# A two-layer diffusion backbone: the next norm's shift and scale move from TensorE, in the attention, to VectorE, at the output projection

## The chip, the cores and the metric

One core of one Trainium2 chip runs the whole program. The metric is the device time of one execution in microseconds (us); three runs of the kernel before are shown, and one further execution was profiled.

## The reference

The even layer is all that the change touches. Its conditioning vector `c` gives six modulation vectors of 1024 values each: shift, scale and gate of the mixer, and shift, scale and gate of the FFN.

```
sh1, sc1, g1, sh2, sc2, g2 = ada_params(c, w_ada[i], b_ada[i])   # silu(c) @ w_ada + b_ada, split in 6
h_lat = modulate(rmsnorm(x_lat, g_mix[i]), sh1, sc1)              # h * (1 + scale) + shift
o_lat, o_ctx = hybrid_mixer(h_lat, h_ctx, ...)                    # attention and Fourier mixing, one output projection
x_lat = x_lat + g1 * o_lat
h = modulate(rmsnorm(x_lat, g_ffn[i]), sh2, sc2)
x_lat = x_lat + g2 * conv_ffn(h, w_up[i], ...)
```

`x` has 512 tokens of 1024 features; the change concerns how `sh2` and `sc2` of layer 0 are computed. All is float32.

## The kernel before

Tokens lie in four row tiles of 128 (`t`), features in eight k tiles of 128 (`kt`). A float32 product is made of three passes on values split into a high and a low part (`mm3`, L222 to L226). Weights of the large products come as 128x1024 chunks in one order through `Stream`: SP loads a chunk into `st` (two buffers), ScalarE casts the high part `whi` (L196), VectorE subtracts to get `wlo` (L197); five chunks are held, and a chunk's buffers come free when TensorE has used it last. The instructions of each engine, and SP's list of loads, stand in an order that a scheduler fixes when the program is built; each engine works its own list from front to back.

The stages around the change, in `mixer` (L889):

- **Attention** (L807): 8 units of a row tile and a key head; in each, four heads with scores (L820), the row maximum on VectorE (L822), the exponential on ScalarE (L825), a division on GpSimd (L828), then transposes of the probabilities (L837), their split into two parts (L290, L291) and the value products (L842).
- Beside it runs a filler, `sums` (L907). For each of gate, shift and scale it makes a `Block` (L320): 8 chunks of `w_ada` (512 KB each, `sa` and `sx`) are loaded in two halves of four, TensorE multiplies each half with the conditioning column `cT` (L340, four groups of 32 output rows), ScalarE and VectorE add the halves in `gs` (L343, L345), and TensorE turns the rows into a column (L350, `col`). The gate's column is spread over all rows (`in_every_row`, L404, L405); shift and scale go to `S2` and `A2` (`in_rows`, L411 and L409), a value for each partition and k tile.
- **Output projection**, `token_major` (L862): the first 512 output columns of all row tiles in one loop over the k tiles (Fourier features first), into the two-bank accumulators `D`; then the last 512 columns, row tile by row tile, into `B`. `residual` (L457) multiplies with the gate and adds to `x` (L460, L461). After each row tile's second half `fin` (L487) normalises it: a sum of squares on ScalarE (L490), the root through L286 on VectorE and L287 on GpSimd, the scaling to `xs` on VectorE (L492). After each pair of row tiles `features` (L469) transposes `xs` on TensorE (L477), applies `A2` and `S2` on ScalarE (L482) and splits the result into `h` on VectorE (L484, L485).
- **FFN** (L939): its first products (`first_blocks`) take the first pair's `h` as it comes. Beside the FFN, other modulation vectors are computed without TensorE: `ada_sum` (L413) loads a chunk of `wada` (L418), and VectorE multiplies it with the activated conditioning row `scb` and sums along it in one instruction (L420). `silu_rows` (L304) makes `scb`: one load to all partitions and a Silu on ScalarE (L307, L308).

`token_major` takes a filler too and runs `n_fill` of its steps after each k tile of the first loop; here it gets none:

```
with sbuf("xs") as xp:
    token_major("wo", (4, 5, 6, 7, 0, 1, 2, 3), gate1, finisher(xp, A2, S2), chain(), 0)
```

The pool `xs` is opened when the attention's pools are closed, and takes their memory.

Of the kernel before, what the change touches and what calls it, by code (L numbers as in the profile page):

```python
# [10 lines left out]
F32 = mybir.dt.float32  # L11
# [6 lines left out]
P = 128  # L18
D = 1024
SEQ = 512  # L20
CTX = 256
KT = D // P
# [199 lines left out]
def mm3(nc, out, lhs, rhs, start, stop):  # L222
    (lh, ll), (rh, rl) = lhs, rhs
    nc.tensor.matmul(out, lhsT=lh, rhs=rh, start=start, stop=False)  # L224
    nc.tensor.matmul(out, lhsT=lh, rhs=rl, start=False, stop=False)  # L225
    return nc.tensor.matmul(out, lhsT=ll, rhs=rh, start=False, stop=stop).ins  # L226
# [3 lines left out]
def tile_hybrid_backbone(ctx: ExitStack, tc: tile.TileContext, x_in, ctx_in, vecs_in, gains_in, cond_in, condT_in, wada, wnat,  # L230
# [10 lines left out]
    def sbuf(name, side="left"):  # L241
        return tc.tile_pool(name=name, bufs=1, side=side, reuse_waits="tile")
# [3 lines left out]
    def nm(s):  # L246
        uid[0] += 1
        return f"{s}_{uid[0]}"

    def bank():  # L250
        return ps.tile([P, 512], F32, tag="B", name=nm("B"), bufs=4)

    def bank2():
        return ps.tile([P, 1024], F32, tag="D", name=nm("D"), bufs=2)
# [14 lines left out]
    gate1 = const.tile([P, D], F32, tag="gate1", name="gate1")  # L269
# [8 lines left out]
    def vec(name, i=0, n=1):  # L278
        o = VEC[name] + i
        return vecs[:, o : o + n]  # L280
# [14 lines left out]
    def hsl(h, kt, a, b):  # L295
        return tuple(h[kt // 4][part][:, kt % 4, a:b] for part in range(2))
# [5 lines left out]
    cur = {}  # L302
# [7 lines left out]


    def chunk_tile():
        return wp.tile([P, D], F32, tag="sa", name=nm("sa"), bufs=3)

    sels = const.tile([P, 4], F32, tag="sels", name="sels")
# [83 lines left out]
    def in_every_row(col, dst, halves=(0, 1)):  # L399
        for half in halves:  # L400
            b = bank()
            for k in range(4):
                kt = 4 * half + k
                nc.tensor.matmul(b[:, k * P : (k + 1) * P], lhsT=col[:, kt : kt + 1].to_broadcast([P, P]), rhs=ident, start=True, stop=True)  # L404
            nc.scalar.copy(dst[:, half * 512 : half * 512 + 512], b)  # L405

    def in_rows(col, dst, gname=None):
        if gname is not None:
            nc.vector.scalar_tensor_tensor(out=dst, in0=col, scalar=1.0, in1=vec(gname, 0, KT), op0=ALU.add, op1=ALU.mult)  # L409
        else:  # L410
            nc.vector.tensor_copy(dst, col)  # L411
# [29 lines left out]
    def chain(*gens):  # L441
        for g in gens:
            yield from g

    def run(gen, n=1):
        for _ in range(n):
            if next(gen, "end") == "end":
                return

    def drain(gen):  # L450
        for _ in gen:
            pass
# [409 lines left out]
    def token_major(key, kts, gate, fin, filler, n_fill):  # L862

        def part(t, kt, w, acc, n):
            mm3(nc, acc, hsl(h, kt, t * P, (t + 1) * P), tuple(u[:, (kt % 2) * 512 : (kt % 2 + 1) * 512] for u in w), n == 0, n == len(kts) - 1)

        D0, D1 = bank2(), bank2()
        acc = [D0[:, 0:512], D0[:, 512:1024], D1[:, 0:512], D1[:, 512:1024]]
        for n, kt in enumerate(kts):
            w = stream.get((key, 0, kt // 2))  # L870
            for t in range(TT):
                part(t, kt, w, acc[t], n)
            if n % 2 == 1:
                stream.release((key, 0, kt // 2))
            run(filler, n_fill)
        drain(filler)
        for t in range(TT):
            residual(t, 0, acc[t], gate)
        for t in range(TT):
            b = bank()  # L880
            for n, kt in enumerate(kts):
                part(t, kt, stream.get((key, 1, kt // 2)), b, n)
            residual(t, 1, b, gate)
            if t == TT - 1:
                for kt in kts[1::2]:
                    stream.release((key, 1, kt // 2))
            fin(t)

    def mixer():  # L889
        A2, S2 = mods[0]  # L890
        with ExitStack() as tables:
            keep = tables.enter_context(sbuf("keep", "right"))
            gain = keep.tile([P, 2, HD], F32, tag="gain", name="gain")
            with sbuf("pre") as pre:
                q_ps, kv_ps, rot = load_and_project(gain, keep, pre)
            with sbuf("qkv") as qkv:
                qT = qkv.tile([P, NQ, SEQ], F32R, tag="qT", name="qT")
                kk = [qkv.tile([P, NKV, SEQ + CTX], F32R, tag=f"kk{i}", name=f"kk{i}") for i in range(2)]
                vv = qkv.tile([P, NKEY, NKV, 2, HD], F32R, tag="vv", name="vv")
                with sbuf("four") as four:  # L900
                    heads_and_fourier(q_ps, kv_ps, rot, gain[:, 1, :], qT, kk, vv, four)
                tables.close()
                with sbuf("att") as ap:
                    ahead = iter((0, 0, 1, 1, 1, 1, 1, 0))
                    uses = ((2, lambda col: in_every_row(col, gate1)), (3, lambda col: in_rows(col, S2)), (4, lambda col: in_rows(col, A2, "gf0")))

                    def sums():  # L907
                        todo = []
                        for j, use in uses:
                            block = Block(j, ap)  # L910
                            todo += [(block, use, 0), (block, use, 1)]
                        for n, (block, use, half) in enumerate(todo):
                            if n == 0:
                                block.load(0)
                                yield
                            block.product(half)
                            if n + 1 < len(todo):
                                todo[n + 1][0].load(todo[n + 1][2])
                            if half == 1:
                                yield  # L920
                                use(block.col())
                            else:
                                yield

                    filler = sums()
                    run(filler)

                    def fill(weights=1):
                        if weights:
                            stream.fill(stream.loaded + next(ahead))  # L930
                        run(filler)

                    attention(qT, kk, vv, ap, fill)
                    drain(filler)
        with sbuf("xs") as xp:
            token_major("wo", (4, 5, 6, 7, 0, 1, 2, 3), gate1, finisher(xp, A2, S2), chain(), 0)


    def ffn(l, filler, filler1, mods, out_dram=None):  # L939
# [329 lines left out]
def _fm(a):  # L1269
    return a.reshape(-1, P).T  # L1270


def _layout(inp):
    w = {k: np.asarray(v) for k, v in inp.items()}
    tb = _tables()
    wall = np.stack([_chunk(w, k) for k in _chunk_order()])
    ba = w["b_ada"]
    parts = [_fm(ba.reshape(-1)), _fm(w["g_mix"][0]), _fm(w["g_mix"][1]),
             _fm(w["g_ffn"][0]), _fm(w["g_ffn"][1]), _fm(w["b_pw1"][0]), _fm(w["ln_g"][0]), _fm(w["ln_b"][0])]
    for l in range(2):  # L1280
        parts.append(w["w_fdw"][l].reshape(3, 2 * NF, P).transpose(2, 1, 0).reshape(P, 6 * NF))
    parts += [_fm(w["b_fdw"][l]) for l in range(2)]
    vecs = np.concatenate(parts, axis=1)
    w0 = w["w_ada"][0].reshape(KT, P, 6, 2, 512)
    w4 = w["w_ada"][0].reshape(KT, P, 6, 4, 256)
    nat = [np.concatenate([w4[2 * c + i][:, 0:2, qd].reshape(P, 512) for i in range(2)], axis=1) for qd in range(4) for c in range(4)]
    nat += [w0[kt][:, j].reshape(P, D) for j in (2, 3, 4) for kt in range(KT)]
    wada = w["w_ada"].reshape(2, D, 6 * KT, P).transpose(0, 2, 3, 1).reshape(12 * KT, P, D)
    wc = np.concatenate([w["w_cdw"][0], w["b_cdw"]])
    return {  # L1290
        "x": w["x"][0],
        "ctx": w["ctx"][0],
        "vecs": vecs,
        "gains": np.stack([w["q_gain"][0], w["k_gain"][0]]),
        "cond": w["c"][0],
        "condT": np.stack([_fm(w["c"][0]), _fm(w["c_ctx"])], axis=2).reshape(P, 2 * KT),
        "wada": wada,
        "wnat": np.stack(nat),
        "wall": wall,
        "wcdw": np.concatenate([wc, wc, wc]),  # L1300
        "bpw2": w["b_pw2"][0],
        "dft": tb["dft"],
        "ch": tb["ch"],
        "rope": tb["rope"],
        "fw": tb["fw"],
        "iv": tb["iv"],
        "vt": tb["vt"],
    }
# [17 lines left out]
```

## Time and profile before

| | |
|---|---|
| median of 3 runs | 1200.55 us (1198.1 to 1201.82) |
| the profiled execution | 1201.3 us, its span 1199.5 us |
| TensorE, products / weight loads | 1158.0 us (97%) / 963.1 us (80%) |
| VectorE | 770.5 us (64%) |
| ScalarE | 521.2 us (43%) |
| GpSimd | 107.2 us (9%) |
| memory traffic over the span | 130 GB/s |

Busy time is the time in which an engine had an instruction in work. TensorE's ends are modelled and overlap with the next product, so that its products are counted by their starts below. In the profile PE is TensorE, PEld its weight loads, DVE VectorE, ACT ScalarE, POOL GpSimd and SP the engine that issues most loads; L12 is line 12 of the kernel.

### The profile page before, as it was taken

How to read it: one execution, taken by the hardware profiler on the slowest of the kernel's cores; microseconds unless marked ns; L12 is line 12 of the kernel's file. 1: busy time of each engine (PE TensorE's matmuls, PEld its weight loads, DVE VectorE, ACT ScalarE, POOL GpSimd, SP SyncE). 2: the span in 40 equal slices, each digit the busy share in tenths (PEclk: the TensorE clock that was granted, in tenths of full speed). 3: DMA queues.
4: the chain of work that ended last, by engine and by line, in shares of the span. 5: the costliest groups of instructions: out<-in, count | busy, mean ns of one | idle time of the engine just before them, and what ended most of it. 6: DMA issues, size and time to landing. Idle time of an engine off the chain costs nothing.

```text
span 1199.5 us, 15250 instructions
## 1 busy us (share of the span) xinstructions
PE 1158.0 (97%) x5849; PEld 963.1 (80%) x5849; DVE 770.5 (64%) x1198; ACT 521.2 (43%) x789; POOL 107.2 (9%) x107
## 2 busy tenths in 40 slices
PE   6999899999999999999999999799999999999998
PEld 4787577889888888888888888688888888888886
DVE  4468679465966666676856875856685555555563
ACT  4455677335533434344434343444544343434341
POOL 0234445000000000000001310000000000000000
PEclk9999899999999999999999999999999999999999
DMA  9742451122644544453624642012262323232330
GB/s 360 255 150 77 152 208 57 53 70 71 210 164 156 172 158 158 158 176 126 224 88 165 209 147 71 22 53 87 87 213 88 98 96 98 96 101 93 95 117 36
DMA packets 43832, 156.41 MB, mean 130 GB/s; under 512 B 5008, under 2 KB 5520, under 8 KB 43504
## 3 DMA queue, kind: packets, MB, share of 16 engines
q1 hardware_dynamic: 42192, 149.51, 36.5%
q0 software_dynamic: 1120, 5.54, 1.3%
q8 instruction: 46, 0.75, 0.2%
q10 hardware_dynamic: 448, 0.39, 0.1%
q14 instruction: 26, 0.21, 0.1%
HBM read 153.33 MB, written 2.10 MB: 130 GB/s over the span
## 4 chain that ended last, share of the span: by engine, by line
PE 88%; DVE 5%; ACT 3%; DMA 2%; issue 1%; POOL 0%; SPq 0%; ACTq 0%; DVEq 0%
PE B L224 20%; PE B L225 20%; PE B L226 20%; PE D L225 7%; PE D L224 7%; PE D L226 7%; PE B L842 2%; PE B L837 1%; PE D L820 1%; DMA st<-in_wall_dram 1%; ACT whi L196 1%; PE B L340 1%; DVE wlo L197 1%; PE D L477 1%; PE B L387 1%
## 5 line engine op out<-in xcount | busy, mean ns | idle before, releaser
L197 DVE TENSOR_TENSOR wlo<-st,whi 128x1024 fp32r<-128x1024 f32 x174 | 212.6, 1223 | 240.5 <-ACT whi L196 240.2
L225 PE MATMUL B<-h,whi 128*128 128x512 f32 (+1 forms) x880 | 320.2, 367 | 0.0
L226 PE MATMUL B<-h,wlo 128*128 128x512 f32 (+1 forms) x880 | 318.6, 366 | 0.0
L224 PE MATMUL B<-h,whi 128*128 128x512 f32 (+1 forms) x880 | 312.2, 367 | 3.6 <-DVE h L484 3.6
L196 ACT CAST whi<-st 128x1024 fp32r<-128x1024 f32 x174 | 182.9, 1052 | 218.5 <-PE B L225 137.1
L225 PEld LDWEIGHTS B<-h,whi 128*128 128x128 f32 x880 | 165.9, 189 | 26.9 <-DVE h L485 0.2
L226 PEld LDWEIGHTS B<-h,wlo 128*128 128x128 f32 x880 | 165.6, 189 | 26.6
L224 PEld LDWEIGHTS B<-h,whi 128*128 128x128 f32 x880 | 161.0, 189 | 31.1 <-DVE h L484 4.5
L290 ACT CAST g<-g 128x512 fp32r<-128x512 f32 x88 | 54.7, 622 | 166.5 <-DVE g L966 88.2
L291 DVE TENSOR_TENSOR g<-g,g 128x512 fp32r<-128x512 f32 x88 | 60.5, 689 | 53.1 <-ACT g L290 51.3
L287 POOL TENSOR_TENSOR tiny<-tiny,mhalf 128x1 f32<-128x1 f32 (+3 forms) x26 | 22.4, 860 | 608.9 <-DVE tiny L286 607.8
L224 PE MATMUL D<-whi,g 128*128 128x512 f32 x176 | 68.5, 389 | 0.0
L225 PE MATMUL D<-wlo,g 128*128 128x512 f32 x176 | 68.5, 389 | 0.0
L224 PE MATMUL B<-whi,g 128*128 128x512 f32 x176 | 68.5, 389 | 0.0
L225 PE MATMUL B<-wlo,g 128*128 128x512 f32 x176 | 68.5, 389 | 0.0
L226 PE MATMUL D<-whi,g 128*128 128x512 f32 x176 | 68.5, 389 | 0.0
L226 PE MATMUL B<-whi,g 128*128 128x512 f32 x176 | 66.8, 389 | 0.0
L420 DVE SCALAR_TENSOR_TENSOR sa<-sa,scb 128x1024 f32<-128x1024 f32 x56 | 66.4, 1220 | 0.4 <-DMA sa<-in_wada_dram 0.4
L956 ACT ACTIVATE tmp<-B,vecs 128x512 f32<-128x512 f32 x84 | 64.7, 772 | 0.0
L958 DVE SCALAR_TENSOR_TENSOR tmp<-B,vecs,tmp 128x511 f32<-128x511 f32 x84 | 62.7, 749 | 2.4
L957 DVE SCALAR_TENSOR_TENSOR tmp<-B,vecs,tmp 128x511 f32<-128x511 f32 x84 | 62.3, 744 | 2.9 <-ACT tmp L956 2.9
L964 ACT ACTIVATE tmp<-tmp 128x512 f32<-128x512 f32 x44 | 27.8, 631 | 82.5 <-DVE tmp L958 82.2
(243 smaller groups left out, 1819.9 us busy)
## 6 DMA issues: line engine op xcount, KB each, us to landing
st<-in_wall_dram SPq DMA_DIRECT2D x174, 512.0 KB, 3.5
sa<-in_wada_dram SPq DMA_DIRECT2D x56, 512.0 KB, 4.2
sa<-in_wnat_dram SPq DMA_DIRECT2D x18, 512.0 KB, 5.2
wn<-in_wnat_dram SPq DMA_DIRECT2D x16, 512.0 KB, 8.2
sx<-in_wnat_dram SPq DMA_DIRECT2D x6, 512.0 KB, 3.5
x<-in_x_dram SPq DMA_DIRECT2D x4, 512.0 KB, 5.3
dft<-in_dft_dram POOLq DMA_DIRECT2D x2, 1024.0 KB, 6.8
out_dram<-x SPq DMA_DIRECT2D x8, 256.0 KB, 2.0
```

Source lines behind the costliest of these rows:

```text
L196: nc.scalar.copy(hi, st)
L197: nc.vector.tensor_tensor(out=lo, in0=st, in1=hi, op=ALU.subtract)
L224: nc.tensor.matmul(out, lhsT=lh, rhs=rh, start=start, stop=False)
L225: nc.tensor.matmul(out, lhsT=lh, rhs=rl, start=False, stop=False)
L226: return nc.tensor.matmul(out, lhsT=ll, rhs=rh, start=False, stop=stop).ins
L290: nc.scalar.copy(hi, src)
L291: nc.vector.tensor_tensor(out=lo, in0=src, in1=hi, op=ALU.subtract)
L420: nc.vector.scalar_tensor_tensor(out=st, in0=st, scalar=1.0, in1=cur["c"], op0=ALU.mult, op1=ALU.mult, accum_out=acc[:, kt : kt + 1])
L956: nc.scalar.activation(out=y, in_=b, func=AF.Identity, scale=w[:, 1:2], bias=vec(f"bfdw{l}", i))
L957: nc.vector.scalar_tensor_tensor(out=y[:, 1:SEQ], in0=b[:, 0 : SEQ - 1], scalar=w[:, 0:1], in1=y[:, 1:SEQ], op0=ALU.mult, op1=ALU.add)
L958: nc.vector.scalar_tensor_tensor(out=y[:, 0 : SEQ - 1], in0=b[:, 1:SEQ], scalar=w[:, 2:3], in1=y[:, 0 : SEQ - 1], op0=ALU.mult, op1=ALU.add)
L964: nc.scalar.activation(out=sa, in_=ya, func=AF.Silu)
```

## The change

The filler of the attention makes the gate only. Shift and scale are made by `ada_rows`, that is, sixteen loads of 512 KB and sixteen sums of 128x1024 on VectorE, by the filler of the output projection, two steps after each k tile of its first loop. Their chunks get eight buffers (`sw`) of their own in the pool `xs`, in which `scb` is made too. The host's array of chunks for the attention shrinks accordingly.

```diff
@@ -310,6 +310,8 @@
     def chunk_tile():
+        if "pool" in cur:
+            return cur["pool"].tile([P, D], F32, tag="sw", name=nm("sw"), bufs=8)
         return wp.tile([P, D], F32, tag="sa", name=nm("sa"), bufs=3)
@@ -902,7 +904,7 @@
                     ahead = iter((0, 0, 1, 1, 1, 1, 1, 0))
-                    uses = ((2, lambda col: in_every_row(col, gate1)), (3, lambda col: in_rows(col, S2)), (4, lambda col: in_rows(col, A2, "gf0")))
+                    uses = ((2, lambda col: in_every_row(col, gate1)),)
@@ -933,7 +935,9 @@
         with sbuf("xs") as xp:
-            token_major("wo", (4, 5, 6, 7, 0, 1, 2, 3), gate1, finisher(xp, A2, S2), chain(), 0)
+            cur["c"], cur["pool"] = silu_rows(xp), xp
+            token_major("wo", (4, 5, 6, 7, 0, 1, 2, 3), gate1, finisher(xp, A2, S2), chain(ada_rows(0, 3, S2), ada_rows(0, 4, A2, "gf0")), 2)
+            del cur["pool"]
@@ -1284,7 +1288,7 @@
-    nat += [w0[kt][:, j].reshape(P, D) for j in (2, 3, 4) for kt in range(KT)]
+    nat += [w0[kt][:, j].reshape(P, D) for j in (2,) for kt in range(KT)]
```

How the lists change, at two places. In the changed program, lines behind L312 stand two further down (L460 is L462 there) and those behind L935 four.

VectorE's list, from the residual of the second row tile to the scaling of the first two, before (`x` is the stream of tokens, `wlo` a low part of a weight chunk, `xs` a normalised row tile):

```order
L460 TENSOR_TENSOR tmp_2546<-B_2521,gate_79 128x512
L461 TENSOR_TENSOR x<-x,tmp_2515 128x512
L197 TENSOR_TENSOR wlo_2504<-st_2505,whi_2503 128x1024
L461 TENSOR_TENSOR x<-x,tmp_2518 128x512
L461 TENSOR_TENSOR x<-x,tmp_2546 128x512
L460 TENSOR_TENSOR tmp_2582<-B_2557,gate_79 128x512
L461 TENSOR_TENSOR x<-x,tmp_2582 128x512
L286 TENSOR_SCALAR tiny_2553<-tiny_2550 128x1
L492 TENSOR_SCALAR xs_2549<-x,tiny_2551 128x1024
```

And now, its end (`sw` is a chunk of `wada`, `asum` the sums, `S` and `A` the shift and the scale; twelve sums stand ahead of these rows and behind the residual of the first pair's first columns, between the operations of the rows above):

```order
L197 TENSOR_TENSOR wlo_2677<-st_2678,whi_2676 128x1024
L197 TENSOR_TENSOR wlo_2683<-st_2684,whi_2682 128x1024
L422 SCALAR_TENSOR_TENSOR sw_2445,asum_2402<-sw_2445,scb_2297 128x1024
L413 COPY S_7_93<-tiny_2399 128x8
L422 SCALAR_TENSOR_TENSOR sw_2466,asum_2402<-sw_2466,scb_2297 128x1024
L422 SCALAR_TENSOR_TENSOR sw_2469,asum_2402<-sw_2469,scb_2297 128x1024
L422 SCALAR_TENSOR_TENSOR sw_2472,asum_2402<-sw_2472,scb_2297 128x1024
L197 TENSOR_TENSOR wlo_2689<-st_2690,whi_2688 128x1024
L197 TENSOR_TENSOR wlo_2695<-st_2696,whi_2694 128x1024
L425 TENSOR_TENSOR tiny_2475<-asum_2402,vecs 128x8
L286 TENSOR_SCALAR tiny_2522<-tiny_2519 128x1
L494 TENSOR_SCALAR xs_2518<-x,tiny_2520 128x1024
```

All sixteen sums, and four splits of FFN weights that stood behind the scaling, now stand ahead of it.

TensorE's list at the first transposes of `xs`, before (`B` is the accumulator of the last row tile's second half):

```order
L226 MATMUL B_2679<-whi_2413,h_85 128x512
L224 MATMUL B_2679<-whi_2413,h_84 128x512
L225 MATMUL B_2679<-wlo_2414,h_84 128x512
L477 MATMUL D_2593<-ident,xs_2549 128x128
L477 MATMUL D_2618<-ident,xs_2549 128x128
L226 MATMUL B_2679<-whi_2413,h_85 128x512
L224 MATMUL B_2679<-whi_2443,h_82 128x512
```

And now (`B_2767` is an accumulator of the FFN):

```order
L225 MATMUL B_2648<-wlo_2419,h_82 128x512
L226 MATMUL B_2648<-whi_2418,h_83 128x512
L479 MATMUL D_2562<-ident,xs_2518 128x128
L479 MATMUL D_2587<-ident,xs_2518 128x128
L479 MATMUL D_2562<-ident,xs_2554 128x128
L479 MATMUL D_2562<-ident,xs_2518 128x128
L224 MATMUL B_2767<-h_82,whi_2460 128x256
```

The transposes stood among the products of the last row tile; now the whole projection stands ahead of them.

## Rows read from the trace of the kernel before

**Rows 1.** The page's busy time, us and share of the span by engine.

```profile
PE 1158.0 (97%) x5849; PEld 963.1 (80%) x5849; DVE 770.5 (64%) x1198; ACT 521.2 (43%) x789; POOL 107.2 (9%) x107
```

**Rows 2.** Stretches: bounds, length, busy us by engine, granted clock, DMA share, GB/s.

```profile
core 0: us, PE busy (x) PEld busy (x) DVE busy (x) ACT busy (x) POOL busy (x), PEclk, DMA share, GB/s
149.70:209.00 59.30, 58.45 (x378) 43.61 (x377) 50.71 (x99) 44.56 (x91) 30.81 (x21) 1.00 0.36 134
200.00:210.00 10.00, 9.98 (x61) 8.18 (x60) 9.77 (x20) 9.01 (x20) 6.37 (x5) 1.00 0.01 2
236.50:262.00 25.50, 25.50 (x120) 21.08 (x119) 14.98 (x26) 7.47 (x11) 1.11 (x2) 1.00 0.16 56
```

**Rows 3.** Timeline, VectorE in the attention: start, us, engine, line, operation.

```profile
149.68 0.96 DVE L822 TENSOR_REDUCE tiny<-D 128x1 f32<-128x768 f32 x1
...
185.21 0.69 DVE L345 TENSOR_TENSOR gs<-B,gs 128x512 f32<-128x512 f32 x1 [0.31 <-PE B L340]
...
194.57 0.93 DVE L822 TENSOR_REDUCE tiny<-D 128x1 f32<-128x768 f32 x1
...
208.94 0.94 DVE L822 TENSOR_REDUCE tiny<-D 128x1 f32<-128x768 f32 x1
```

**Rows 4.** The chain of work in the attention: start, us, what.

```profile
149.39 1.78 PE B L404 x16
151.18 1.85 PE B L340 x16
...
171.19 0.79 PE B L350 x8
```

**Rows 5.** Timeline, TensorE, from the last value product into the FFN.

```profile
236.12 0.39 PE L842 MATMUL B<-pt,vv 128*128 128x512 f32 x1
...
262.13 0.48 PE L224 MATMUL B<-h,whi 128*128 128x256 f32 x2
...
265.24 0.50 PE L224 MATMUL B<-h,whi 128*128 128x256 f32 x2 [1.45 <-DVE h L484]
...
275.93 1.04 PE L477 MATMUL D<-ident,xs 128*128 128x128 f32 x8
277.68 0.50 PE L224 MATMUL B<-h,whi 128*128 128x256 f32 x2 [0.72 <-DVE h L484]
```

**Rows 6.** Timeline, VectorE at the end of the output projection.

```profile
239.58 1.29 DVE L461 TENSOR_TENSOR x<-x,tmp 128x512 f32<-128x512 f32 x2
245.62 1.29 DVE L460 TENSOR_TENSOR tmp<-D,gate 128x512 f32<-128x512 f32 x2 [4.75 <-PE D L226]
246.82 0.68 DVE L460 TENSOR_TENSOR tmp<-B,gate 128x512 f32<-128x512 f32 x1
247.42 0.69 DVE L461 TENSOR_TENSOR x<-x,tmp 128x512 f32<-128x512 f32 x1
248.02 1.22 DVE L197 TENSOR_TENSOR wlo<-st,whi 128x1024 fp32r<-128x1024 f32 x1
249.15 1.29 DVE L461 TENSOR_TENSOR x<-x,tmp 128x512 f32<-128x512 f32 x2
...
251.72 0.15 DVE L286 TENSOR_SCALAR tiny<-tiny 128x1 f32<-128x1 f32 x1
...
254.09 0.76 DVE L492 TENSOR_SCALAR xs<-x,tiny 128x1024 f32<-128x1024 f32 x1 [0.74 <-POOL tiny L287]
```

**Rows 7.** Timeline, VectorE, two sums of the FFN's filler in a row.

```profile
312.74 1.22 DVE L420 SCALAR_TENSOR_TENSOR sa<-sa,scb 128x1024 f32<-128x1024 f32 x1
313.88 0.08 DVE L420 DVE_READ_ACCUMULATOR sa<-sa,scb 128x1 f32 x1
313.88 1.22 DVE L420 SCALAR_TENSOR_TENSOR sa<-sa,scb 128x1024 f32<-128x1024 f32 x1
315.03 0.08 DVE L420 DVE_READ_ACCUMULATOR sa<-sa,scb 128x1 f32 x1
```

**Rows 8.** Timeline, ScalarE: the last cast of the attention, and the conditioning row.

```profile
238.05 0.41 ACT L290 CAST h<-tmp 128x256 fp32r<-128x256 f32 x1 [0.92 <-DVE tmp L850]
...
285.74 1.28 ACT L308 ACT_TABLE_LOAD   x1
288.23 1.06 ACT L308 ACTIVATE scb<-scb 128x1024 f32<-128x1024 f32 x1 [1.20 <-DMA scb<-in_cond_dram]
```

**Rows 9.** Stretches around a gap of TensorE, at the attention's start.

```profile
122.00:123.00 1.00, 0.07 (x1) 0.07 (x1) 1.00 (x3) 0.62 (x1) 0.00 (x0) 1.00 0.00 0
127.00:130.00 3.00, 3.00 (x12) 1.50 (x16) 3.00 (x5) 1.38 (x3) 2.08 (x2) 0.50 0.02 5
130.00:131.00 1.00, 1.00 (x12) 0.12 (x4) 0.16 (x1) 0.81 (x2) 0.85 (x1) 0.90 0.00 0
```

**Rows 10.** Loads of line L418 (512 KB each), from issue to landing.

```profile
DMA to landing us min/median/max: 3.3/4.2/5.6
```

## The prediction

> **What bounds the kernel now.** I read the page's table of busy time first: TensorE is busy for 97% of the span and VectorE for 64% [rows 1]. Such averages say little of one place, and the change touches two: the attention, which loses work, and the stretch from the output projection to the first product of the FFN, which gains it. So I cut the span into these by the view of stretches [rows 2]. From 149.7 to 209.0 TensorE is busy for 58.5 of 59.3 us, but VectorE for 50.7 too. From 236.5 to 262.0 TensorE has no gap at all, and VectorE works 15.0 of 25.5.
>
> Next, how near the attention is to a second limit. The reduction for the maximum (L822) runs once for each head of each row tile, 32 times. From 149.68 to 194.57 there are 15 steps, 2.99 us each; from 194.57 to 208.94, with no product for shift or scale left, 6 steps of 2.395 [rows 3]. That second rate is what other engines allow when these products are gone: VectorE was busy for 9.8 of the 10 us from 200 to 210 [rows 2], so it is near the floor. A busy TensorE is thus not the whole bound.
>
> Behind the attention TensorE is the bound. Its last value product starts at 236.12. From there to the FFN's first product at 262.13 are 26.0 us, filled with 108 products of the projection and 12 transposes for the next norm [rows 5]. The transposes cost 0.11 each by the eight at 275.93, so the projection itself ends 24.7 after the last value product. I count from that product in what follows ("+24.7").
>
> **What is removed.** Four half blocks of products with the modulation's weights, 1.85 each, and two columns of 0.79 go from TensorE: 9.0 us. The gate's two halves, its column and its spread over rows (1.78, of which 1.5 lie behind 149.68) stay [rows 4]. Were TensorE alone the bound, 9.0 would be gained. At the rate of rows 3 without products the 21 steps from 149.68 to 208.94 need 21 x 2.395 = 50.3, and the gate's 1.5 on top give 51.8 instead of 59.26. **I take 7.5.** VectorE's work would be 48.7 of those 51.8, once two additions of the half blocks (L345, 0.69 each) and a few small operations are gone, about 2.0 in all, and 94% is a share that it has reached. Upper end 9.0; lower end 4.3, half of the 8.6 us in which VectorE now idles there, if in-order queues keep the rest. The 16 loads that leave the attention cost nothing there, since SP's list reaches the gate's loads as before. After the last scores, to +0, TensorE runs the same products as before and keeps its time.
>
> **What is added, and where it lands.** Sixteen sums of 128x1024 on VectorE. The loop issues two per k tile, but their data decide. The scheduler puts the second load behind the last value product, whose operands lie where the new tiles are to lie, and the first sum behind the residual of the first two row tiles. So all sixteen come after +0, beside the second half of the projection, and all sixteen stand on VectorE in front of the first L286 of the next norm.
>
> One sum costs 1.145 from start to start [rows 7].
>
> As a duration the row says 1.22, and the Trainium skill (VectorE: DVE Perf Modes, The TRN2 errata) would have 1.224 for 1024 elements by its formula for a two-tensor fp32 operation; by that price the thirteen sums below would take 1.0 longer. The start-to-start of the row decides, because the write's tail overlaps the next instruction.
>
> *When they start.* VectorE ends the first residual at 240.87, which is +4.75 [rows 6]. The Silu of the conditioning row must be done: behind the cast that ends at 238.46 ScalarE loads a table (1.28) and runs it (1.06) [rows 8], done at about 240.8. No wait results. The loads of sums two to eight are issued at +0, and a load lands in 3.3 to 5.6 [rows 10]; so the data are there. *The first three are free:* before, VectorE idles there 4.75 until the second pair of accumulators is complete at 245.62 (+9.5) [rows 6], and three sums take 3.4.
>
> *The rest isn't.* From +9.5 to L286, VectorE's list now has 13 sums (14.9), eight residual operations (0.60 each, 4.8), five splits of weights (L197, 1.14 each, 5.7; before, one stood here) and four small ones (0.4): 25.8. L286 starts at +35.3. Before, it started at 251.72, +15.6 [rows 6]. The splits of FFN weights wait for buffers that TensorE frees during the last row tile, at about +20 to +25, and the queue reaches them only at +26 and later: no further delay. Loads nine to sixteen need a buffer that a sum has freed; sums are 1.145 apart or more, each load half a megabyte, and the last one is issued at about +21 and used at +32. DMA is not the limit. The FFN's third weight tile, queued on SP among these loads, needs a buffer that TensorE frees at about +22: nothing lost.
>
> *What TensorE does.* It ends the projection at +24.7, as nothing there waits for the sums. Its next instruction is the transpose of the normalised row tile. From L286 to the end of the second L492 it took 251.72 to 254.85, 3.1 [rows 6]; so +38.4. From the transposes to the first FFN product it took 1.75 at 275.93 [rows 5]; two of eight transposes can go earlier, so 1.5. The FFN starts at +39.9 instead of +26.0: **13.9 later**, about 12 of it an empty TensorE.
>
> *Two smaller terms.* After such a gap the clock falls: from 122 to 123 TensorE was busy for 0.07 us, and from 127 to 130, when it was busy throughout, the granted clock was 0.50, the lower level of 1.2 GHz; from 130 to 131 it was 0.90 [rows 9]. About 3.2 us at half speed do the work of 1.6, so 1.6 are lost; ends 0 (VectorE's casts may pace the first FFN products anyway) and 3.2. And one wait goes: before, TensorE stood 1.45 for h at 265.24 [rows 5], behind a split on VectorE that is now done earlier.
>
> The sum: 13.9 + 1.6 - 1.45 - 7.5 = **+6.55**. The profiled execution took 1201.3 (span 1199.5), so 1207.85; the median of the runs shown, 1200.55, lies 0.75 below it, which gives **1207.1 us**. A change under 0.3% can't be told from none in a measurement of this kernel.
>
> **Rivals.** *Most is given back:* the attention gains all 9.0 and the clock costs nothing: 13.9 - 1.45 - 9.0 = +3.45, 1204.0, at the edge of no difference. For it speaks a TensorE busy for 98% in the attention; against it VectorE's 50.7 us.
>
> *Worse:* the attention yields only 4.3, sums take 1.30 (1.22 and the 0.08 of reading the accumulator, not overlapped, 2.0 in all for thirteen), the clock takes 3.2: 13.9 + 2.0 + 3.2 - 1.45 - 4.3 = +13.35, 1213.9. That the order of an attention scheduled anew may fit worse speaks for it; the row's even start-to-start against it.
>
> *Faster:* the sums hide in VectorE's idle time, and the 9.0 remain: 1201.3 - 9.0 - 0.75 = 1191.6. It turns on one place: the list between the second residual and L286. Where that ends before TensorE has emptied the projection, nothing is lost; it would have to shrink from 25.8 to 12 or so (24.7 less 9.5, less the 3.1 of the norm). Rows 2 speak for it only on average: VectorE idles 10.5 of the 25.5 us, less than sixteen sums need (18.3).
>
> The Trainium skill (Perfetto Trace Analysis, Identifying the Most-Contended Engine) takes the engine with the highest occupancy as the one to relieve, TensorE by its weight loads; at 80% against VectorE's 64% this change would be a gain. By that rule the time is the 1191.6 of this rival; the stretches of rows 2 and 6 say that the order on VectorE, not its occupancy, decides here.
>
> *The change doesn't do what it says,* in the sense that two sums per k tile don't run beside these k tiles, is part of my forecast and not a case of its own.
>
> **Chances.** The forecast 0.73, given back 0.12, worse 0.10, faster 0.05. The order on VectorE is fixed in the program, so the sign is nearly certain; the sizes aren't. The range goes from 1203.5 to 1214: the two neighbours' times, 1204.0 and 1213.9, with a little at the ends for runs that differ. Slower by over 0.3% (above 1204.2) is the forecast and the worse case, 0.83; within 0.3% the one given back, 0.12; faster 0.05.
>
> **What would show it.** In the changed profile: the steps of L822 (now L824) near 2.4 to 2.5 us from the point where the gate is done, and the last value product near 228.6; sixteen sums in a nearly solid VectorE stretch of some 30 us; TensorE empty for about 12 us in front of the first transposes, released by L494 on VectorE, with the lower clock behind it; the FFN's first product near 268.5. Wrong would be: TensorE's gap under 6 us, or a wait for a load of sw in front of the sums, or an attention that isn't shorter.

## The result, and the profile after

The changed kernel takes **1207.95 us** (median of 5 runs, 1207.68 to 1209.97), the kernel before on the same chip 1200.55 (5 runs): ratio 1.0065, 95% interval 1.0051 to 1.0080, that is 6 to 10 us slower. Timed again it took 1208.06 against 1199.60 (ratio 1.0074, interval 1.0059 to 1.0089). The forecast was 1207.1.

Line numbers are those of the kernel that is shown: L822 is now L824, L842 L844, and in later runs they move again by a few lines. The page's busy time, to be held against [rows 1]:

```profile
PE 1149.7 (95%) x5769; PEld 958.0 (79%) x5769; DVE 786.1 (65%) x1228; ACT 521.0 (43%) x788; POOL 108.2 (9%) x107
```

TensorE works 8.3 us less, VectorE 15.6 more, and the span is 6.4 longer (1205.9). Where that arises is seen in stretches (columns as in [rows 2]): the attention from the 11th to the 32nd reduction, the next 26 us, the rest of the projection, and the gap behind it.

```profile
146.62:200.84 54.22, 51.48 (x300) 40.59 (x299) 50.38 (x95) 43.80 (x90) 30.81 (x21) 1.00 0.01 1
200.84:226.84 26.00, 26.00 (x131) 21.50 (x130) 11.76 (x19) 9.64 (x15) 2.93 (x2) 1.00 0.12 41
227.60:252.40 24.80, 24.80 (x110) 20.26 (x108) 22.42 (x39) 7.65 (x9) 0.00 (x0) 1.00 1.01 395
252.45:268.17 15.72, 2.24 (x10) 1.44 (x9) 12.66 (x24) 4.09 (x6) 1.11 (x2) 0.64 0.50 173
```

The attention's 21 steps take 54.22 instead of 59.26 [rows 3]. In the last stretch TensorE works 2.24 of 15.72 us; no such stretch was there before [rows 2, 5]. What VectorE did meanwhile, from its timeline:

```profile
231.04 1.28 DVE L463 TENSOR_TENSOR x<-x,tmp 128x512 f32<-128x512 f32 x2
233.63 1.23 DVE L422 SCALAR_TENSOR_TENSOR sw<-sw,scb 128x1024 f32<-128x1024 f32 x1 [1.30 <-DMA sw<-in_wada_dram]
...
237.25 1.28 DVE L462 TENSOR_TENSOR tmp<-D,gate 128x512 f32<-128x512 f32 x2
...
258.21 1.22 DVE L422 SCALAR_TENSOR_TENSOR sw<-sw,scb 128x1024 f32<-128x1024 f32 x1
259.35 0.09 DVE L422 DVE_READ_ACCUMULATOR sw<-sw,scb 128x1 f32 x1
259.35 1.23 DVE L422 SCALAR_TENSOR_TENSOR sw<-sw,scb 128x1024 f32<-128x1024 f32 x1
...
260.50 2.56 DVE L197 TENSOR_TENSOR wlo<-st,whi 128x1024 fp32r<-128x1024 f32 x2
262.98 0.16 DVE L425 TENSOR_TENSOR tiny<-asum,vecs 128x8 f32<-128x8 f32 x1
263.05 0.15 DVE L286 TENSOR_SCALAR tiny<-tiny 128x1 f32<-128x1 f32 x1
...
265.42 0.75 DVE L494 TENSOR_SCALAR xs<-x,tiny 128x1024 f32<-128x1024 f32 x1 [0.74 <-POOL tiny L287]
```

From 233.63 to 263.05 it hardly stops (29.3 of 29.4 us busy): 16 sums, 1.14 to 1.15 from start to start, among residual operations and splits. The last value product now starts at 227.59 ("+0"), so the first L286 comes at +35.5. TensorE, from its timeline:

```profile
264.68 0.69 PE L479 MATMUL D<-ident,xs 128*128 128x128 f32 x2 [12.23 <-DVE tiny L286]
266.23 1.54 PE L479 MATMUL D<-ident,xs 128*128 128x128 f32 x6 [0.86 <-DVE xs L494]
268.17 0.80 PE L224 MATMUL B<-h,whi 128*128 128x256 f32 x2 [0.39 <-DVE h L486]
...
283.52 0.74 PE L224 MATMUL B<-h,whi 128*128 128x256 f32 x4 [0.71 <-DVE h L486]
```

It waits 12.23 us in front of the first transposes; six transposes then take 1.54, where eight took 1.04 [rows 5]. The granted clock is 0.64 of full speed over the last stretch above, and 0.50, the lower level, from 264.68 to 268.17. The FFN starts at +40.6.

**A comparison that holds for all runs.** The first reduction of the attention starts at 120.67 in the profile of before and at 117.16 in this one, though nothing ahead of it was changed. So the profiles are compared by four parts: up to the first reduction, from there to the last (32 in all), from the last to the FFN's first product, and from there to the end. Before, these were 120.67, 88.27, 53.19 and 937.4; after, 117.16, 83.68, 67.33 and 937.7. The change thus costs 14.1 behind the attention and gains 4.6 in it (14.2 and 5.8 in the second profiles of both, below); the 3.5 of the first part are looked into below.

### The profile page after: what moved, and what is told of

It reads as the page before. It is cut to its first block, busy times and chain, and to the rows that moved or that the text cites. A ratio compares the mean times of both kernels' runs of the same rounds, so it can differ in the third digit from the quotient of the medians.

```text
span 1205.9 us, 15115 instructions
## 1 busy us (share of the span) xinstructions
PE 1149.7 (95%) x5769; PEld 958.0 (79%) x5769; DVE 786.1 (65%) x1228; ACT 521.0 (43%) x788; POOL 108.2 (9%) x107
## 4 chain that ended last, share of the span: by engine, by line
PE 85%; DVE 7%; ACT 3%; DMA 2%; issue 2%; POOL 0%; SPq 0%; ACTq 0%; DVEq 0%; POOLq 0%
PE B L224 20%; PE B L225 20%; PE B L226 20%; PE D L225 7%; PE D L224 7%; PE D L226 7%; DVE sw L422 1%; PE B L844 1%; DVE tiny L824 1%; ACT whi L196 1%; PE B L839 1%; DVE wlo L197 1%; PE D L479 1%; DMA st<-in_wall_dram 1%; PE B L389 1%
## 5 line engine op out<-in xcount | busy, mean ns | idle before, releaser
L224 PE MATMUL B<-h,whi 128*128 128x512 f32 (+1 forms) x880 | 313.3, 368 | 2.5 <-DVE h L486 2.5
L224 PEld LDWEIGHTS B<-h,whi 128*128 128x128 f32 x880 | 161.7, 189 | 30.3 <-DVE h L486 3.7
L224 PE MATMUL D<-whi,g 128*128 128x512 f32 x176 | 68.5, 389 | 0.0
L224 PE MATMUL B<-whi,g 128*128 128x512 f32 x176 | 68.5, 389 | 0.0
L968 ACT ACTIVATE tmp<-tmp 128x512 f32<-128x512 f32 x44 | 27.8, 632 | 82.4 <-DVE tmp L962 82.2
```

What stands on the lines that cost most here:

```text
L968: nc.scalar.activation(out=sa, in_=ya, func=AF.Silu)
```

## The experiments

My theory: attention and projection are two separate terms, and the second comes from what stands on VectorE in front of the first L286. Rivals: the loads in front of the FFN's weights make the gap; the attention's gain doesn't last; each sum has a fixed price wherever it stands.

**The attention alone, and the sums alone.** First the changed kernel without its sums:

```
-            cur["c"], cur["pool"] = silu_rows(xp), xp
-            token_major(..., chain(ada_rows(0, 3, S2), ada_rows(0, 4, A2, "gf0")), 2)
-            del cur["pool"]
+            in_rows(vec("ba", 3 * KT, KT), S2)
+            in_rows(vec("ba", 4 * KT, KT), A2, "gf0")
+            token_major(..., chain(), 0)
```

> Left out: the shift's and scale's sums over the conditioning row with their loads, the row's load and its Silu; the next norm gets the bias terms alone. The attention is that of the changed kernel. Theory (the two parts are separate, and what the attention gains stays gained when nothing is put in front of the next norm): last value product at about 227.6 as in the changed kernel (236.12 before), FFN's first product 26.0 after it as before, time 1200.6 - 8.5 = 1192. Rival (the earlier end of the attention only moves the wait: the FFN's weights or the residual are then late): TensorE stands 4 us or more in front of the FFN, time 1196 or more. Second rival (the attention does not gain by itself): 1199 to 1201.

1195.18 against 1199.97: ratio 0.9960 (0.9941 to 0.9978), 2.6 to 7.1 us faster. First to last reduction 83.55, last reduction to FFN 52.69. TensorE has no gap from the last value product to the FFN (columns as in [rows 2]):

```profile
226.83:252.82 25.99, 25.99 (x123) 21.55 (x121) 14.98 (x26) 7.47 (x11) 1.12 (x2) 1.00 0.19 60
```

So the attention gains by itself and keeps it, but less than the 8.5 expected: these were read from two absolute times, 236.12 and 227.59, which hold the 3.5 us of the first part too. The second rival is out; of the first one no wait is to be seen.

Then the kernel before with sixteen sums added to the projection (`chunk_tile` as in the change, results into tiles that nothing reads):

> Kernel before, its products for shift and scale kept in the attention, and the sixteen loads and sums added to the output projection (their result is not used). Theory (costs add up): the last value product stays near 236.1, the FFN's first product moves from 26.0 to 40.6 behind it, time 1200.6 + 14.6 = 1215, 14.2 to 15.5 over before. Rival (part of the 14.6 is there only because the attention of the changed kernel ends earlier, in front of loads that would have come anyway): 1208 to 1211.

1213.80 against 1199.97: 1.0116 (1.0097 to 1.0135), 13.8 us slower, just under the 14.2 to 15.5 of the theory. Last reduction to FFN 68.38, which is 15.2 more than before; TensorE waits 12.83 for L286. The two terms add up: -4.8 and +13.8 make +9.0, within the interval of the whole change. The rival (1208 to 1211) is out: the fastest run took 1212.43.

**The sums' time on VectorE against their loads.**

```
+                m = 8 if "pool" in cur else D
-                nc.vector.scalar_tensor_tensor(out=st, in0=st, ...)
+                nc.vector.scalar_tensor_tensor(out=st[:, :m], in0=st[:, :m], ...)
```

> Changed kernel, each of the sixteen sums taken over 8 of its 1024 columns: the rest of the sum is left out, while the loads, the waits and the number of instructions stay. Theory (VectorE's list in front of the first L286 sets the FFN's start): some 13 us of that list go; what is left of it waits for the loads, sixteen half megabytes at the 420 GB/s that the changed kernel shows there, the last one landing about 22 us after the last value product; the FFN's first product 27 to 30 after it instead of 40.6, time 1193 to 1197. Rival (the loads of sw, 8 MB in front of the FFN's weights on one queue, set the end): TensorE's gap stays near 12 us, time 1205 to 1208.

1200.71, no difference to before (1.0009, 0.9996 to 1.0021): neither expectation. Last reduction to FFN 60.47. The sums now take 0.17, and yet the end of VectorE's list was not free:

```profile
254.00 0.17 DVE L423 SCALAR_TENSOR_TENSOR sw<-sw,scb 128x8 f32<-128x8 f32 x1 [1.05 <-DMA sw<-in_wada_dram]
254.09 0.08 DVE L423 DVE_READ_ACCUMULATOR sw<-sw,scb 128x1 f32 x1
255.26 0.17 DVE L423 SCALAR_TENSOR_TENSOR sw<-sw,scb 128x8 f32<-128x8 f32 x1 [1.09 <-DMA sw<-in_wada_dram]
255.35 0.08 DVE L423 DVE_READ_ACCUMULATOR sw<-sw,scb 128x1 f32 x1
255.47 0.17 DVE L426 TENSOR_TENSOR tiny<-asum,vecs 128x8 f32<-128x8 f32 x1
255.56 0.15 DVE L286 TENSOR_SCALAR tiny<-tiny 128x1 f32<-128x1 f32 x1
```

And the stretch from the last value product to the last load's landing (columns as in [rows 2]):

```profile
227.78:255.50 27.72, 24.87 (x110) 20.27 (x108) 14.71 (x53) 8.70 (x11) 0.00 (x0) 1.00 1.01 394
```

DMA is full for all of it, at 394 GB/s; 8.4 of the 10.9 MB are the sixteen chunks, the rest is the conditioning row and weights. The loads by themselves hold L286 back to 27.8 behind the last value product, VectorE's list to 35.5. So there are **two limits, one close behind the other**: about half of the 14 us would stay with sums that cost nothing.

**Half of the sums.** The shift by eight sums, the scale by products as before:

```
-                    uses = ((2, ...),)
+                    uses = ((2, ...), (4, lambda col: in_rows(col, A2, "gf0")))
...
-            token_major(..., chain(ada_rows(0, 3, S2), ada_rows(0, 4, A2, "gf0")), 2)
+            token_major(..., ada_rows(0, 3, S2), 2)
```

> Changed kernel with half of the change: the shift by eight sums, the scale by products in the attention as before. Theory (only what stands on VectorE in front of the first L286 beyond the time that TensorE needs for the projection costs anything): the attention gains half, 4.3; the list loses eight sums (9.2) and, as placed now, three of the splits (3.4), so the first L286 comes at 22 to 23 behind the last value product instead of 35.5, and the FFN starts 27.5 to 28.5 behind it; time 1198 to 1199, a little under before. Rival (each sum has its price, so half the sums cost half): 4.3 gained and 7.3 lost, 1203.6. Second rival (all sums hide, occupancy decides): 1196.

1200.90, no difference (1.0003, 0.9992 to 1.0015), between the theory and the rival of a fixed price. The first L286 came at 255.59, 21.7 behind the last value product (233.86), but two splits now stand behind the two L286, each in front of its L494, and the second L494 comes only at 259.85. The FFN starts 29.2 behind the last value product, where 27.5 to 28.5 was expected. First to last reduction 86.27 (2.0 gained, not 4.3), last reduction to FFN 55.88 (2.7 lost).

**The norm first.** Is it the place of L286? Four sums stay in front; the other twelve are queued behind the second L494 (`done` below), and must be over only before the transposed rows are scaled:

```
             done = nc.vector.tensor_scalar(out=xn, in0=x[:, t, :], scalar1=r, ...).ins
+            if t == 1 and rest is not None:
+                cur["turn"] = done
+                drain(rest)
...
+            run(both, 4)    # both: the filler with the sixteen sums
```

> Changed kernel, same sums and loads, one thing moved: twelve of the sixteen sums stand on VectorE behind the norm of the first two row tiles (L286 and L494) instead of in front of it, so that they hold up only the scaling of the transposes. Theory (VectorE's work, not the place of L286, sets when scale and shift are there): the second xs comes some 20 us earlier and the transposes are done long before, but the last sum stays near 36 behind the last value product, with two splits in front of the scale; the FFN's first product 37 to 39.5 after the last value product instead of 40.6, time 1204.5 to 1207.5. Rival (the wait of L286 alone makes the loss): 27 to 30 after it, 1196 to 1199. The loads alone would allow about 30, by the run with short sums.

1207.15, 1.0053 (1.0037 to 1.0069): as slow as the change. VectorE, and then TensorE, from their timelines:

```profile
248.43 0.75 DVE L494 TENSOR_SCALAR xs<-x,tiny 128x1024 f32<-128x1024 f32 x1 [0.74 <-POOL tiny L287]
...
264.05 1.22 DVE L422 SCALAR_TENSOR_TENSOR sw<-sw,scb 128x1024 f32<-128x1024 f32 x1
...
265.27 2.35 DVE L197 TENSOR_TENSOR wlo<-st,whi 128x1024 fp32r<-128x1024 f32 x2
267.54 0.15 DVE L425 TENSOR_TENSOR tiny<-asum,vecs 128x8 f32<-128x8 f32 x1
267.73 0.17 DVE L411 SCALAR_TENSOR_TENSOR A<-tiny,vecs 128x8 f32<-128x8 f32 x1
```

```profile
253.33 0.82 PE L479 MATMUL D<-ident,xs 128*128 128x128 f32 x6
268.94 0.79 PE L224 MATMUL B<-h,whi 128*128 128x256 f32 x2 [14.09 <-DVE h L486]
```

Counted from the last value product (229.06), the second L494 comes 18 us earlier than in the changed kernel (19.4 against 37.8) and the transposes run at 253.33, and TensorE waits 14.09 for the scale instead. From 249.10, where the twelve sums begin, to 268.94 VectorE is busy for 19.1 of 19.8 us and waits for no load. So not the place of L286 but the work, too much of it between the last value product and the FFN, which starts 39.9 behind that product. The same move with the shift alone:

> Only the shift by eight sums (scale by products in the attention), and four of these eight behind the norm of the first two row tiles. Theory: with half the sums VectorE and the loads both fit beside the projection, so with the norm in front nothing waits: the FFN's first product 26 to 27.5 behind the last value product (29.2 with the sums in front), the attention as in the run with the shift alone, time 1197.5 to 1199. Rival (splits of the FFN's weights, behind the late sums, set the FFN's start instead): 29, time 1200 to 1201.

1198.99 against 1200.21, 0.9993 (0.9982 to 1.0004). The time lies at the upper end of the theory's range, but can't be told from before, nor from the run without the move. Last reduction to FFN is 55.15 instead of 55.88, the FFN's start 28.4 behind the last value product, between theory and rival, and TensorE still waited 2.60 for h. By the times it is undecided. VectorE's timeline shows what the shift waited for:

```profile
256.57 1.22 DVE L422 SCALAR_TENSOR_TENSOR sw<-sw,scb 128x1024 f32<-128x1024 f32 x1
...
257.71 2.35 DVE L197 TENSOR_TENSOR wlo<-st,whi 128x1024 fp32r<-128x1024 f32 x2
259.99 0.16 DVE L425 TENSOR_TENSOR tiny<-asum,vecs 128x8 f32<-128x8 f32 x1
```

Behind the last sum two splits of weights (2.3 us together) stand in front of the operation that ends the shift, as the rival says; they make up most of the 2.60. No run takes them out.

**The same sums, earlier.** From the last reduction on VectorE has room (11.76 of 26 us busy, above). The sums couldn't use it, since their loads came too late. SP's list in the changed kernel, then SP's waits there and in the run with the sums alone (who waits for whom, us, times, longest):

```profile
226.72 0.33 SPq L195 DMA_DIRECT2D st<-in_wall_dram  x1
227.10 0.42 SPq L307 DMA_DIRECT2D scb<-in_cond_dram  x1
227.58 0.42 SPq L420 DMA_DIRECT2D sw<-in_wada_dram  x1
```

```profile
SPq L195 <- DVE wlo L197: 7.8, 1, 7.8
```

```profile
SPq L195 <- DVE wlo L197: 7.3, 1, 7.3
SPq L420 <- PE B L844: 0.2, 1, 0.2
```

The conditioning row and the first chunk stand right behind a weight load that waits more than 7 us for a buffer of `st`; in the run with the sums alone the first chunk then waits 0.2 us more for a value product, as `sw` takes over memory of the attention. The place in SP's list and the shared memory thus hold the loads to nearly the same point, and no run takes one away without the other. The next run changes both: the loads go through the three buffers of `sa`, and the conditioning row takes the place of `sx`, in a pool that lives on:

```
+                side = tables.enter_context(sbuf("side", "right"))
...
-                t = ... self.pool.tile([P, D], F32, tag="sx", ...)
+                t = ... self.side.tile([P, D], F32, tag="sx", ...)
...
-            cur["c"], cur["pool"] = silu_rows(xp), xp
-            token_major(..., 2)
+            cur["c"] = silu_rows(side, "sx", last)    # behind the last exponential
...
+                token_major(..., 4)
```

> Changed kernel with all sixteen sums, put elsewhere: their loads go through the three buffers of sa, which are free once the gate's products are done, and the conditioning row takes the fourth block's buffer (moved to a pool of its own, which stays open through the projection), so nothing has to wait for the last value product. Silu behind the last exponential. VectorE is busy for 11.9 of the 26 us from 200 to 226 in the changed kernel, and DMA for 0.12: the sums find room there. Theory (place decides, not the number of sums): the last sum ends near the last value product, L286 comes at about 16 behind it as in the kernel before, the FFN's first product 26 behind it; time as with the attention alone, 1194 to 1197. Rival (sums between the splits of the probabilities on VectorE keep TensorE waiting in the value products): the last value product 3 to 8 us later than with the attention alone, 1198 to 1203.

**1190.87 against 1200.21**, 0.9921 (0.9904 to 0.9938): 7.4 to 11.5 us faster than before, the best of all, and 3 under the expected range. The profile is that of the fastest of its six runs (1188.11). First to last reduction 79.89, last reduction to FFN 53.17, as before. The 26 us behind the last reduction, then VectorE and TensorE:

```profile
197.11:223.11 26.00, 26.00 (x131) 21.56 (x130) 21.85 (x40) 11.89 (x17) 2.94 (x2) 1.00 0.68 217
```

```profile
201.66 1.23 DVE L421 SCALAR_TENSOR_TENSOR sa<-sa,scb 128x1024 f32<-128x1024 f32 x1 [2.21 <-ACT scb L309]
...
231.59 1.23 DVE L421 SCALAR_TENSOR_TENSOR sa<-sa,scb 128x1024 f32<-128x1024 f32 x1 [0.23 <-DMA sa<-in_wada_dram]
...
244.09 0.15 DVE L286 TENSOR_SCALAR tiny<-tiny 128x1 f32<-128x1 f32 x1 [0.68 <-ACT xs L491]
```

```profile
248.53 1.03 PE L478 MATMUL D<-ident,xs 128*128 128x128 f32 x8
250.28 0.50 PE L224 MATMUL B<-h,whi 128*128 128x256 f32 x2 [0.71 <-DVE h L485]
```

VectorE does 10 us more in the same 26 (21.85 against 11.76), and TensorE still works all of them. L286 no longer waits for a sum. The rival's delay is there too: the last value product comes 30.1 behind the last reduction instead of 26.7. But TensorE runs products of the projection in between, so that nothing is lost, and the FFN follows 23.1 behind the last value product instead of 26. The price of a sum, with its load, is its place.

The attention came out 3.8 us shorter than in the changed kernel, which the sums don't explain. The buffer of `sx`, the fourth chunk of each half block, might: it now has a pool of its own, and its first load was issued at 80.27 instead of 113.47, and the gate's first products ran at 118.93 instead of 125.01. Two runs take that alone, the pool for `sx` in the kernel before and in the changed one:

> Kernel before with one thing changed: the fourth load of a block of weights (sx) lies in a pool of its own instead of in memory that the stage ahead of the attention still uses, as in the run with the sums early. No sum is added and no product removed. Theory (this is a gain by itself, and some 4 of the 9.3 us by which the run with the sums early beats the kernel before belong to it): the gate's first products start before the attention's first reduction instead of 8 us behind it, the time from the first to the last reduction falls from 88.3 to about 84.5, the granted clock from 120 to 135 rises from 0.77 to 1.00, time 1195 to 1197.5. Rival (all of that gain came from the sums' place): 1199 to 1201.

> Changed kernel with sx in a pool of its own and nothing else; the sums stand where the change puts them. Theory: the same 3.5 to 4.5 us as in the kernel before, and the loss behind the projection stays whole: last reduction to the FFN's first product 67 (53 with the sums early), time 1203 to 1204.5, so that the place of the sums alone is worth 12 to 14 us between this kernel and the one with the sums early. Rival (the loss shrinks with the earlier attention): under 1200.

1196.31 against 1199.60 (0.9974, 0.9962 to 0.9985) and 1204.96 (1.0045, 1.0032 to 1.0058): each some 3 us under its own kernel. From 120 to 135, in the first and in the second:

```profile
120.00:135.00 15.00, 12.13 (x59) 6.17 (x58) 8.79 (x17) 7.80 (x15) 5.09 (x4) 0.77 0.54 199
```

```profile
120.00:135.00 15.00, 10.61 (x61) 5.34 (x61) 10.10 (x20) 8.88 (x18) 5.87 (x4) 1.00 0.57 200
```

In the second the attention is shorter, 80.16 from the first to the last reduction, with the clock at 1.00. In the first it isn't, 87.85 with a clock of 0.77, against the theory's 84.5 and 1.00: that profile belongs to the longest of its nine runs. Their times go with the mean granted clock of the run: 1194.3 to 1194.9 at 0.997, 1196.1 to 1198.6 at 0.995, and 1198.7 and 1199.0 at 0.993, where the kernel before took 1198.8 to 1200.1. So the gain comes together with a clock that falls less; in which stage stays open. With the buffer in both, the place of the sums is worth 14.1 us by the medians (1204.96 to 1190.87, from two sets of runs in which the kernel before took 1199.60 and 1200.21), and 14.2 in the part from the last reduction to the FFN (67.41 to 53.17).

**What is chance.** Both kernels a second time, unchanged:

> Kernel before, not changed, for a second profile. In the first one the attention's first reduction (L822) started at 120.67, in the changed kernel at 117.16, though nothing in front of it was changed; the granted clock from 92 to 120 was 0.94 in the one and 1.00 in the other. Theory (which of the two a run gets is chance, and belongs to no kernel): anything from 116.5 to 121; with a clock of 1.00 from 92 to 120 it lies near 117 to 119. Rival (it belongs to the kernel before): 120 to 121 again, with 0.94. The attention from the 11th to the 32nd reduction takes 59.0 to 59.5 by both.

> Changed kernel, unchanged, a second time. The difference of the two first profiles (span 6.4) holds 3.5 us from stages ahead of the attention, which the change doesn't touch; without them it is 9.9. Theory (that 3.5 is a matter of the single run): the median stays 6 to 9.5 over the kernel before, the first reduction starts anywhere from 116.5 to 121.5. Rival (it belongs to the program): 117 again.

The first reduction starts at 121.27 and 121.88, both a little later than either theory allowed. For the kernel before alone this would fit the rival too. But the changed kernel went from 117.16 to 121.88, and the run with the sums alone, which changes nothing up to the end of the attention, started at 116.76: the first part belongs to the run. The granted clock goes with it. From 92 to 116, ahead of the attention (columns as in [rows 2]), it was 0.93 in both profiles of before; in the changed kernel and in that again:

```profile
92.00:116.00 24.00, 23.11 (x114) 18.86 (x113) 22.23 (x35) 14.52 (x26) 12.27 (x9) 1.00 0.26 89
```

```profile
92.00:116.00 24.00, 22.39 (x100) 18.49 (x101) 21.45 (x36) 12.01 (x21) 13.70 (x10) 0.93 0.14 44
```

Over all thirteen profiles the first reduction starts at 116.58 to 119.17 where that clock is 1.00 (eight), and at 120.67 to 121.88 where it is 0.93 (five). The other parts of the repeats: 88.24, 53.22 and 938.8 for before, 82.44, 67.41 and 937.1 for after. The 11th to the 32nd reduction took 59.31 and 54.23, within 0.1 of the first profiles. The expectation of the changed kernel's time held, 1208.06.

## Why the prediction was right, and where it was off

- **The place of the loss: right.** Second residual forecast at +9.5, seen at +9.66; first L286 at +35.3, seen at +35.5; second xs at +38.4, seen at +38.6; TensorE empty for about 12 us, seen 12.2; FFN at +39.9, seen at +40.6. The 13.9 were 14.6, and 14.7 between the two repeats. Of the missing 0.7, 0.2 are there at the second xs; the other 0.5 lie in the transposes, taken at the duration of [rows 5], which here ran at the lower clock.
- **"No wait results": wrong, with next to no effect.** A wait for a load of `sw` in front of the sums was named as a sign of being wrong, and it came. The first sum waited 1.30 for its load, as the conditioning row and the chunks behind it are all asked for at about +0; it came at +6.0 instead of +4.75, nearly all within idle time that was free anyway: behind the third sum the next residual starts at +9.66, where +9.5 was forecast.
- **"DMA is not the limit": right for this kernel, and for too weak a reason.** A load's latency was compared with the time until its use; the rate counts. With short sums the loads alone hold L286 to 27.8. So the condition of the rival *faster*, a list shrunk to 12 us, was not enough: the loads would have had to go too.
- **Clock and wait, +0.15: right within 0.4.** From the FFN's first product to its next wait at L224 [rows 5, the last one] it was 15.55 us before and 15.35 after (268.17 to 283.52): -0.2. The wait of 1.45 went, and TensorE was busy for 1.25 longer (14.64 instead of 13.39), at a clock of 0.92 instead of 1.00.
- **The attention, 7.5: too much.** It is 5.0 from the 11th to the 32nd reduction, in both pairs of profiles, and 5.4 with the 0.4 gained from there to the last value product. Two readings failed. The 9.0 came from the lengths of two pieces of the chain [rows 4]; TensorE's busy time fell by 6.9 (58.4 to 51.5), so a half block with its share of the columns is worth 1.7. And the floor of 2.395 was read over six steps, which are not whole units of four heads. In the changed kernel the units repeat in 9.95 us (180.94 to 190.89), 2.49 a step, which gives 21 x 2.49 + 1.5 = 53.8 for the 54.22 measured:

```profile
180.94 0.93 DVE L824 TENSOR_REDUCE tiny<-D 128x1 f32<-128x768 f32 x1
...
183.21 0.95 DVE L824 TENSOR_REDUCE tiny<-D 128x1 f32<-128x768 f32 x1
...
185.31 0.95 DVE L824 TENSOR_REDUCE tiny<-D 128x1 f32<-128x768 f32 x1
...
187.73 0.94 DVE L824 TENSOR_REDUCE tiny<-D 128x1 f32<-128x768 f32 x1
...
190.89 0.94 DVE L824 TENSOR_REDUCE tiny<-D 128x1 f32<-128x768 f32 x1
```

The sum with the measured terms is 14.6 - 0.2 - 5.4 = +9.0, where +6.55 was forecast. The medians give +7.4 and +8.5. The place and the way of the loss were foreseen, but that the 1207.1 came out 0.9 from the first median is in part luck: one of its terms was 7.5 instead of 5.4, and the medians' differences are 0.5 to 1.6 less than what the terms add up to. The 6.4 between the first two profiles look still closer, but 3.5 of that are the chance of the first part.

The Trainium skill (VectorE: DVE Perf Modes, The TRN2 errata) would have 1.224 for a sum, an estimate by its formula for two fp32 tensors. As a duration the trace agrees (1.22); but sums in a row start 1.14 to 1.15 apart (258.21 and 259.35, and the next operation at 260.50), and by that, the start-to-start of [rows 7], the list on VectorE came out right.

The Trainium skill's rule in Perfetto Trace Analysis, Identifying the Most-Contended Engine, gave the rival at 1191.6. The changed kernel, at 1207.95, speaks against it as a forecast. With the sums in VectorE's free time the run took 1190.87, but some 3 us of that gain are the other buffer's: the move itself is then worth some 6 us, not the 9.0 of that rival, and only where the order allows it.

## What to carry to other kernels

Work moved to an engine with idle time costs nothing only where that time lies between the moment its data can be there and the moment its result is needed. Look first at what delays the data. Here it was no lack of VectorE's or DMA's time over the span but memory shared with the stage before, and a place in SP's list behind a load that waited. Other buffers and an earlier place turned 7 us lost into 9 gained, some 3 of them by a buffer that the sums don't need. Before relieving one limit, price the next one behind it, here the loads' rate, and read a rate over whole periods of the loop.

## What was not expected of the hardware

- The granted clock ahead of the attention differs between runs of the same program: the changed kernel had 1.00 from 92 to 116 in one profile and 0.93 in the other, and its first reduction started at 117.16 and 121.88. A difference of two single profiles is uncertain by that much, and should be read part by part.
- Sixteen loads of 512 KB, issued within 21 us (227.58 to 248.4), took 8.2 us from issue to landing (median), against 3.3 to 5.6 for the loads of [rows 10], at a DMA share of 1.01 and 395 GB/s.
- A sum over 8 columns takes 0.17 and its accumulator's read 0.08, against 1.22 and 0.08 over 1024: nearly all of the cost of these sums is in the columns.
